# A streaming encoder step in split float32: hi and lo part of an operand as one 512-column moving operand in the first half of the tokens

## Chip, cores, metric

The kernel runs on one core of one Trainium2 chip. The metric is device time in microseconds. The kernel before took 2561.59 us, the median of 3 runs (2561.55 to 2563.88).

## What is computed

One inference step of an encoder with model width 1024 for 512 prompt tokens and 32 sample tokens, all float32. There are two layers, and each is a SwiGLU feed-forward network (FFN), a token mixer, and a second FFN, with RMSNorm and modulation around each:

```python
x = x + HALF * mod[:, 2, None] * rms_norm(swiglu(h, w_ffn_in[l, 0], w_ffn_out[l, 0]), g_norm[l, 1])
...   # the mixer: retention in layer 0, differential attention in layer 1
x = x + HALF * mod[:, 8, None] * rms_norm(swiglu(h, w_ffn_in[l, 1], w_ffn_out[l, 1]), g_norm[l, 5])
...   # after layer 0: one shared K/V projection of x

def swiglu(h, w_in, w_out):
    a, b = jnp.split(h @ w_in, 2, axis=-1)
    return (jax.nn.silu(a) * b) @ w_out
```

`w_ffn_in` is 1024 x 5632, `w_ffn_out` 2816 x 1024. Retention has a 1024 x 6144 input and a 2048 x 1024 output projection, K/V 1024 x 2048, the attention's query and output 1024 x 1024 each. The modulation vectors `mod` come from matrix-vector products with 1024 x 9216 weights for each layer.

## The kernel before

**Layout.** Activations lie transposed, features on the 128 partitions and tokens along the free dimension. The 544 tokens are cut into two halves, H = 0 with 256 columns and H = 1 with 288 (`COLS`, L28). Both halves go through all stages.

**Split float32.** A product of float32 values is made of three fp32r matmuls: a weight is split into w_hi (a cast, L578) and w_lo (the rest, L581), an operand into x_hi and x_lo (for instance L929 and L930), and w_hi x_hi + w_hi x_lo + w_lo x_hi is accumulated in one PSUM bank.

**Units.** A unit is one block of 128 output features with 6 or 8 k-tiles of 128 input features. There are 368 units in program order: 272 in the four FFNs, 64 in retention, 16 in shared K/V, 8 for queries, 8 for the attention's output. `run_unit` (L587) runs one unit for one half: per k-tile it waits for the operand (L593) and issues three matmuls at L599. Then the unit's `post` process takes the result from the bank and gives the bank back (`put_bank`). A half's run of an 8-tile unit is 24 matmuls. The `post` processes are: in an FFN `post_a` (Silu at L953 for layer 0, Tanh and a multiply at L949 and L950 for layer 1) and `post_b` (L965 or L962, then `split_ops`, L929 and L930); in `out_stage` a ScalarE copy (L916) for the first third of the inner dimension and a VectorE add (L918) for the others; rotary products (`rot`, L1021 and L1025); copies of values (L1074, L1375); gates (L1095). An FFN runs in three parts: 8, 8 and 6 pairs of `post_a` and `post_b` units, each followed by 8 output units that need the operands of that part.

**Memory.** Operand parts lie in `SLOT` (L346): 34 tiles for each half, of 256 or 288 columns, and an operand takes two of them (L686). Everything else of changing life is cut from an arena `FA` of 20600 columns. Banks: 5 of 8 for units (`MAINB`), 3 for the rest. Four weight buffers (`NW`), three for raw weights (`NRAW`).

**Order.** `Sched` simulates the engines with assumed costs (`c_r`, `c_act`, `c_dvp` and others, L243) and so fixes, before the launch, the order in which each engine's instructions are issued. Where several are ready, the lowest priority number goes first: post processes have 20 or 15, normalisation 1 to 2 (`x_norm`, `pre_ops`), a unit's matmuls 1000 plus their place in the order, the modulation matmuls (L504) `ADA_HI` = 900 once their due unit is reached, weight casts and subtractions `CONV_P` and `FIN_P` = 0.

`plan` (L636) merges the two halves' units into one order of 736 places along a path. A pair (a, b) of the path says how many units the first and the second half have done. The path is set by hand: `BND` (L62) at the joins between sub-layers up to layer 1's first FFN, `ATT` (L64) from there on, both in offsets from a stage's first unit. Mostly the halves alternate, the first one unit ahead; near joins it is some units ahead, and in layer 1 up to some 60. `plan` also decides on weight loads: where the halves of a unit are close together, one load and one split serve both (`Load(u, 2)`), elsewhere each half loads its own. `launch` (L621) goes through the order, waits for the unit's split weights, and takes a bank.

**Joins.** After the last output unit of a sub-layer, `sub_end` (L845) makes squares (L824), their sum (L828), a mean over partitions by TensorE (L711), a power on GpSimd (L717), a broadcast by TensorE (L722), the scaled sum into X (L877, L880), and `x_norm` and `pre_ops` make the next operands (L749, L758, L764). Meanwhile TensorE has the other half's units.

All loads and stores are DMAs issued by SyncE (`nc.sync`, L394). The rotary tables are loaded when unit `ROPE_LEAD` = 30 before the stage is launched.

Of the kernel before, what the change touches and what calls it, by code (L numbers as in the profile page):

```python
# [49 lines left out]
def _path():  # L50
# [3 lines left out]
    for e in ((0, 1), (0, 2), "kv", (1, 0)):  # L54
# [216 lines left out]
class Operand:  # L271
# [51 lines left out]
def yoco_step(ctx: ExitStack, tc: tile.TileContext, I, O):  # L323
# [19 lines left out]
    NHALF = sb("NHALF", [P, 4])  # L343
    LAM = sb("LAM", [P, 12])
    GSUB = sb("GSUB", [P, 1])
    SLOT = [[sb(f"r{H}_{i}", [P, COLS[H].stop - COLS[H].start], F32R) for i in range(NSLOT[H])] for H in range(2)]  # L346
    WT = [sb(f"w{i}", [P, 2, 8, P], F32R) for i in range(NW)]
    AN = ARENA_N
    FA = sb("FA", [P, AN])
# [237 lines left out]
    def run_unit(u, H, b):  # L587
        c = COLS[H]
        n = c.stop - c.start
        d = u.load[H]  # L590
        for k in range(u.nk):
            op = u.ops[k]
            yield op.ev[H]  # L593

            def mm(k=k, op=op):
                hi, lo = op.hi(H), op.lo(H)
                w = WT[d.w]
                for j, (a, x) in enumerate(((0, hi), (0, lo), (1, hi))):
                    te.matmul(PS[b][:, :n], lhsT=w[:, a, k, :], rhs=x,  # L599
                                     start=(k == 0 and j == 0), stop=(k == u.nk - 1 and j == 2))  # L600
            yield pe(3 * c_r(n), mm)
        d.users -= 1
        if d.users == 0:
            S.put(wpool, d.w)
        u.stage.left[H] -= 1
        if u.stage.left[H] == 0:
            for op in u.stage.ops:
                for t in op.part[H]:
                    S.put(slots[H], t)
        go(u.post(H, b), 20)  # L610
# [71 lines left out]
    def ensure(op, H):  # L682
        if op.part[H] is None:
            if op.asked[H] is None:
                op.asked[H] = Ev()
                op.part[H] = yield ("get", slots[H], 2)  # L686
                S.set(op.asked[H])
            else:
                yield op.asked[H]
# [243 lines left out]
    def ffn(l, j, hops, yevs):  # L933
        w_in, w_out = I["w_ffn_in"][l][j], I["w_ffn_out"][l][j]
        parts = ((0, 8), (8, 16), (16, 22))
        for pi, (f0, f1) in enumerate(parts):
            st = Stage(hops if pi == 2 else [])
            gops = [Operand() for _ in range(f1 - f0)]
            for f in range(f0, f1):
                sil = {}  # L940
                sev = (Ev(), Ev())

                def post_a(H, b, sil=sil, sev=sev):
                    n = COLS[H].stop - COLS[H].start
                    t = yield from get(n)
                    sil[H] = t
                    if l in TANH:

                        yield act(n, lambda: nc.scalar.activation(fa(t), PS[b][:, :n], AF.Tanh, scale=0.5))  # L949
                        yield dvp(n, lambda: nc.vector.scalar_tensor_tensor(fa(t), fa(t), 1.0, PS[b][:, :n], ALU.add,  # L950
                                                                            ALU.mult))
                    else:
                        yield act(n, lambda: nc.scalar.activation(fa(t), PS[b][:, :n], AF.Silu))  # L953
                    put_bank(b)
                    S.set(sev[H])

                def post_b(H, b, sil=sil, sev=sev, op=gops[f - f0]):
                    n = COLS[H].stop - COLS[H].start
                    yield sev[H]
                    t = sil[H]  # L960
                    if l in TANH:
                        yield dvp(n, lambda: nc.vector.scalar_tensor_tensor(fa(t), PS[b][:, :n], 0.5, fa(t), ALU.mult,  # L962
                                                                            ALU.mult))
                    else:
                        yield dvp(n, lambda: nc.vector.tensor_tensor(fa(t), PS[b][:, :n], fa(t), ALU.mult))  # L965
                    put_bank(b)
# [47 lines left out]
    def rot(H, b, rr, dst, pr=20, m=0):  # L1014
# [6 lines left out]
        yield dvp(n, lambda: nc.vector.tensor_tensor(a1, PS[b][:, :n], fa(rr, n, c.start), ALU.mult), pr)  # L1021

        def sw():
            for x, y in ((0, 64), (64, 0)):
                nc.vector.tensor_tensor(fa(t1, n, n, x, x + 64), PS[b][y:y + 64, :n],  # L1025
                                        fa(rr, n, NTOK + c.start, y, y + 64), ALU.mult)
        yield ("DVE", 2 * c_dvp(n), sw, pr)
        put_bank(b)
# [11 lines left out]
    def retention(hops, yevs):  # L1040
# [8 lines left out]
        for h in range(8):  # L1049
# [40 lines left out]
            def post_g(H, b, hd=hd, h=h, j=0):  # L1090
# [262 lines left out]
    def shared_kv(hops):  # L1353
# [3 lines left out]
        for h in range(8):  # L1357
# [604 lines left out]
```

## Time and profile before

| | |
|---|---|
| median of 3 runs | 2561.59 us (2561.55 to 2563.88) |
| the profiled execution | 2562.68 us |
| its span, first to last instruction | 2560.9 us |
| mean granted TensorE clock | 0.993 |
| instructions | 48166 |
| matmul instructions, of them at L599 | 19848, 17280 |
| DMA | 404.61 MB, mean 158 GB/s |

The profile is of one execution, taken by the hardware. PE is TensorE's matmuls, PEld its weight loads (they overlap PE), DVE is VectorE, ACT ScalarE, POOL GpSimd, SP SyncE. Matmuls are pipelined, so one's duration overlaps the next one's. In tiles' names `ps` is a PSUM bank, `w` a split weight buffer, `r` an operand part, `FA` the arena. A clock of 1.00 is the full 2.4 GHz, 0.5 is 1.2 GHz.

### The profile page before, as it was taken

How to read it: one execution, taken by the hardware profiler on the slowest of the kernel's cores; microseconds unless marked ns; L12 is line 12 of the kernel's file. 1: busy time of each engine (PE TensorE's matmuls, PEld its weight loads, DVE VectorE, ACT ScalarE, POOL GpSimd, SP SyncE). 2: the span in 40 equal slices, each digit the busy share in tenths (PEclk: the TensorE clock that was granted, in tenths of full speed). 3: DMA queues.
4: the chain of work that ended last, by engine and by line, in shares of the span. 5: the costliest groups of instructions: out<-in, count | busy, mean ns of one | idle time of the engine just before them, and what ended most of it. 6: DMA issues, size and time to landing. Idle time of an engine off the chain costs nothing.

```text
span 2560.9 us, 48166 instructions
## 1 busy us (share of the span) xinstructions
PE 2496.2 (97%) x19848; PEld 2379.2 (93%) x19848; DVE 1400.1 (55%) x2604; ACT 1091.3 (43%) x2159; POOL 58.5 (2%) x88
## 2 busy tenths in 40 slices
PE   7999999999999999999999999999899999999998
PEld 5889999899999997999998899999699988898998
DVE  5223334955424457323338944555786987768555
ACT  4222224643333355322126533444565655465434
POOL 0000000000000000000000000000000000000000
PEclk9999999999999999999999999999899999999999
DMA  8662323642222237522226853555655445545553
GB/s 321 263 239 84 98 90 107 227 152 95 80 80 91 76 109 279 189 88 95 91 76 221 271 173 127 167 180 190 241 194 175 159 160 185 178 161 169 165 165 109
DMA packets 122235, 404.61 MB, mean 158 GB/s; under 512 B 15008, under 2 KB 33568, under 8 KB 111776
## 3 DMA queue, kind: packets, MB, share of 16 engines
q1 hardware_dynamic: 122016, 401.54, 45.9%
q8 instruction: 155, 2.54, 0.4%
q14 instruction: 64, 0.52, 0.1%
HBM read 388.25 MB, written 13.24 MB: 157 GB/s over the span
## 4 chain that ended last, share of the span: by engine, by line
PE 86%; DVE 8%; ACT 3%; issue 2%; DMA 1%; POOL 0%; SPq 0%; POOLq 0%; DVEq 0%; ACTq 0%
PE ps L599 77%; DVE w L581 2%; PE ps L504 2%; ACT w L578 1%; DVE FA L1025 1%; DVE FA L749 1%; DVE r L764 1%; PE ps L1601 1%; PE ps L1231 1%; PE ps L1219 1%; ACT FA L858 0%; PE ps L1540 0%; DMA X<-in_xb 0%; PE ps L1594 0%; DVE FA L828 0%
## 5 line engine op out<-in xcount | busy, mean ns | idle before, releaser
L599 PE MATMUL ps<-r,w 128*128 128x256 f32 (+1 forms) x17280 | 2269.4, 291 | 15.8 <-ACT r L758 11.5
L599 PEld LDWEIGHTS ps<-r,w 128*128 128x128 f32 x17280 | 2205.5, 191 | 55.7 <-issue 25.9
L581 DVE TENSOR_TENSOR w<-FA,w 128x1024 fp32r<-128x1024 f32 (+1 forms) x552 | 658.9, 1194 | 572.4 <-ACT w L578 567.5
L578 ACT CAST w<-FA 128x1024 fp32r<-128x1024 f32 (+1 forms) x552 | 564.6, 1023 | 883.5 <-PE ps L599 799.8
L965 DVE TENSOR_TENSOR FA<-ps,FA 128x256 f32<-128x256 f32 (+1 forms) x88 | 38.8, 441 | 192.5 <-PE ps L599 191.9
L929 ACT CAST r<-FA 128x288 fp32r<-128x288 f32 (+1 forms) x176 | 73.1, 416 | 107.3 <-DVE FA L965 88.3
L918 DVE TENSOR_TENSOR FA<-ps,FA 128x288 f32<-128x288 f32 (+1 forms) x144 | 62.3, 438 | 97.7 <-PE ps L599 96.2
L930 DVE TENSOR_TENSOR r<-FA,r 128x288 fp32r<-128x288 f32 (+1 forms) x176 | 76.6, 437 | 21.9 <-ACT r L929 21.5
L758 ACT ACTIVATE r<-FA,MOD 128x256 fp32r<-128x256 f32 (+1 forms) x168 | 63.1, 437 | 51.7 <-DVE FA L749 51.3
L828 DVE TENSOR_TENSOR FA<-FA 128x256 f32<-128x256 f32 (+1 forms) x168 | 73.1, 436 | 12.7 <-ACT FA L824 11.1
L504 PE MATMUL ps<-FA,SC 128*32 128x512 f32 x576 | 70.7, 605 | 5.6 <-DMA FA<-in_ada 5.6
L962 DVE SCALAR_TENSOR_TENSOR FA<-ps,FA 128x288 f32<-128x288 f32 (+1 forms) x88 | 38.4, 439 | 49.9 <-PE ps L599 49.8
L953 ACT ACTIVATE FA<-ps 128x256 f32<-128x256 f32 (+1 forms) x88 | 34.5, 393 | 69.7 <-PE ps L599 69.6
L749 DVE SCALAR_TENSOR_TENSOR FA<-X,DRV,ps 128x256 f32<-128x256 f32 (+1 forms) x168 | 57.3, 396 | 9.5 <-PE ps L722 9.3
L717 POOL TENSOR_TENSOR FA<-FA,NHALF 128x2 f32<-128x2 f32 (+1 forms) x24 | 21.7, 906 | 1774.8 <-DVE FA L715 1687.0
L858 ACT ACTIVATE FA<-FA,DRV 128x256 f32<-128x256 f32 (+1 forms) x144 | 59.1, 442 | 2.9
L764 DVE SCALAR_TENSOR_TENSOR r<-FA,MOD,r 128x256 fp32r<-128x256 f32 (+1 forms) x168 | 58.5, 400 | 0.4 <-ACT r L758 0.2
L1025 DVE TENSOR_TENSOR FA<-ps,FA 64x288 f32<-64x288 f32 (+1 forms) x128 | 56.1, 438 | 2.0
L916 ACT COPY FA<-ps 128x288 f32<-128x288 f32 (+1 forms) x96 | 36.3, 380 | 44.6 <-PE ps L599 44.6
L1021 DVE TENSOR_TENSOR FA<-ps,FA 128x256 f32<-128x256 f32 (+1 forms) x64 | 27.8, 437 | 48.9 <-PE ps L599 48.8
L504 PEld LDWEIGHTS ps<-FA,SC 128*32 128x32 f32 x576 | 14.8, 109 | 33.6 <-issue 22.4
L824 ACT ACTIVATE FA<-FA 128x256 f32<-128x256 f32 (+1 forms) x84 | 35.7, 425 | 15.5 <-DVE FA L918 14.9
(149 smaller groups left out, 1120.6 us busy)
## 6 DMA issues: line engine op xcount, KB each, us to landing
FA<-in_w_ffn_in SPq DMA_DIRECT2D x261, 512.0 KB, 3.3
FA<-in_ada SPq DMA_DIRECT2D x80, 1024.0 KB, 7.1
FA<-in_w_ffn_out SPq DMA_DIRECT2D x95, 512.0 KB, 3.5
FA<-in_w_in_a SPq DMA_DIRECT2D x58, 512.0 KB, 3.2
FA<-in_w_ffn_out SPq DMA_DIRECT2D x62, 384.0 KB, 3.1
FA<-in_w_kv SPq DMA_DIRECT2D x24, 512.0 KB, 4.4
FA<-in_w_out_a SPq DMA_DIRECT2D x20, 512.0 KB, 3.6
FA<-in_w_q_b SPq DMA_DIRECT2D x16, 512.0 KB, 3.4
```

The source lines that it names most:

```text
L504: te.matmul(PS[b][32 * g:32 * g + 32, :], lhsT=SC[:, k, :], rhs=fa(ada_buf[u, k], 512, g * 512), start=(k == 0), stop=(k == 7))
L578: yield act(n, lambda: nc.scalar.copy(hi, src))
L581: yield dve(n, lambda: nc.vector.tensor_tensor(lo, src, hi.bitcast(F32), ALU.subtract))
L599: te.matmul(PS[b][:, :n], lhsT=w[:, a, k, :], rhs=x, start=(k == 0 and j == 0), stop=(k == u.nk - 1 and j == 2))
L749: nc.vector.scalar_tensor_tensor(fa(z, c1 - c0, o), X[:, f, c0:c1], DRV[:, gi, f, s:s + 1], PS[Rb][:, o:o + c1 - c0], ALU.mult, ALU.mult)
L758: nc.scalar.activation(op.hi(H, c0, c1), fa(z, c1 - c0, o), AF.Identity, bias=MOD[:, mi, f, s:s + 1])
L764: nc.vector.scalar_tensor_tensor(op.lo(H, c0, c1), fa(z, c1 - c0, o), MOD[:, mi, f, s:s + 1], op.hi(H, c0, c1).bitcast(F32), ALU.add, ALU. ...
L828: yield dve(n, lambda: nc.vector.tensor_tensor(acc, acc, fa(t), ALU.add))
L918: yield dvp(n, lambda: nc.vector.tensor_tensor(Y[:, f, c], PS[b][:, :n], Y[:, f, c], ALU.add), 15)
L929: yield act(n, lambda: nc.scalar.copy(op.hi(H), src), pr)
L930: yield dve(n, lambda: nc.vector.tensor_tensor(op.lo(H), src, op.hi(H).bitcast(F32), ALU.subtract), pr)
L1025: nc.vector.tensor_tensor(fa(t1, n, n, x, x + 64), PS[b][y:y + 64, :n], fa(rr, n, NTOK + c.start, y, y + 64), ALU.mult)
```

## The change

In the first half (H = 0) the two parts of an operand lie side by side in one tile of 2 x 256 columns. Per k-tile, one matmul of w_hi takes both as a moving operand of 512 columns, and one matmul of w_lo takes x_hi with 256 columns. A bank then holds two partial results. `result` adds them: a ScalarE copy of the right half, then a VectorE add of the left half. `out_stage` past the first third adds both halves to its target with two VectorE adds. The post processes of H = 0 work on the sum in the arena. H = 1 is as before. The offsets of the order, the number of slots (17 double ones in place of 34), and some priorities and leads are set anew.

```diff
-BND = {(0, 1): (7, 7, 6, 10), (0, 2): (7, 7, 6, 5), 'kv': (8, 8, 6, 8), (1, 0): (0, 1, 4, 6)}
+BND = {(0, 1): (7, 7, 7, 12), (0, 2): (8, 9, 10, 7), 'kv': (8, 9, 10, 8), (1, 0): (7, 0, 4, 0)}
-ATT = [(Q, -67, Q, -75), (Q, 4, Q, -34), (Q, 8, Q, -23), (OB, 0, Q, -31), (OB, -8, Q, -13), (F2, 1, Q, -16),
-       (F2, -6, Q, 0), (F2, 6, Q, -2), (F2, 37, OB, -1), (F2, 55, OB, 1), (F2, 55, F2, 0), (F2, 70, F2, -4)]
-NSLOT = (34, 34)
+ATT = [(Q, -64, Q, -67), (Q, 0, Q, -40), (Q, 8, Q, -24), (OB, -16, Q, -32), (OB, -8, Q, -18), (F2, 1, Q, -26),
+       (F2, -12, Q, 0), (F2, 7, Q, 0), (F2, 26, OB, -2), (F2, 59, OB, 3), (F2, 47, F2, 1), (F2, 73, F2, -5)]
+NSLOT = (17, 17)
...
             def mm(k=k, op=op):
-                hi, lo = op.hi(H), op.lo(H)
                 w = WT[d.w]
-                for j, (a, x) in enumerate(((0, hi), (0, lo), (1, hi))):
-                    te.matmul(PS[b][:, :n], lhsT=w[:, a, k, :], rhs=x,
-                                     start=(k == 0 and j == 0), stop=(k == u.nk - 1 and j == 2))
-            yield pe(3 * c_r(n), mm)
+                first, last = k == 0, k == u.nk - 1
+                if H:
+                    for j, (a, x) in enumerate(((0, op.hi(H)), (0, op.lo(H)), (1, op.hi(H)))):
+                        te.matmul(PS[b][:, :n], lhsT=w[:, a, k, :], rhs=x, start=first and j == 0,
+                                  stop=last and j == 2)
+                else:
+                    te.matmul(PS[b][:], lhsT=w[:, 0, k, :], rhs=op.part[H][:].rearrange("p s n -> p (s n)"),
+                              start=first, stop=False)
+                    te.matmul(PS[b][:, :n], lhsT=w[:, 1, k, :], rhs=op.hi(H), start=False, stop=last)
+            yield pe(3 * c_r(n) if H else c_r(n) + c_r(2 * n), mm)
...
+    def result(b, dst, pr=None):
+
+        yield act(256, lambda: nc.scalar.copy(dst, PS[b][:, 256:]), pr)
+        yield dvp(256, lambda: nc.vector.tensor_tensor(dst, PS[b][:, :256], dst, ALU.add), pr)
+        put_bank(b)
...
-                if first:
-                    yield act(n, lambda: nc.scalar.copy(Y[:, f, c], PS[b][:, :n]), 15)
+                if H == 0 and first:
+                    yield from result(b, Y[:, f, c], 15)
                 else:
-                    yield dvp(n, lambda: nc.vector.tensor_tensor(Y[:, f, c], PS[b][:, :n], Y[:, f, c], ALU.add), 15)
-                put_bank(b)
+                    if first:
+                        yield act(n, lambda: nc.scalar.copy(Y[:, f, c], PS[b][:, :n]), 15)
+                    else:
+                        def add():
+                            for o in range(0, 512 - 256 * H, 256):
+                                nc.vector.tensor_tensor(Y[:, f, c], PS[b][:, o:o + n], Y[:, f, c], ALU.add)
+                        yield ("DVE", (2 - H) * c_dvp(n), add, 15)
+                    put_bank(b)
...
                 def post_a(H, b, sil=sil, sev=sev):
                     n = COLS[H].stop - COLS[H].start
                     t = yield from get(n)
                     sil[H] = t
+                    src = PS[b][:, :n]
+                    if H == 0:
+                        s = yield from get(n)
+                        src = fa(s)
+                        yield from result(b, src)
...
-ROPE_LEAD = 30
+ROPE_LEAD = 38
...
-FIN_P = 0
-CONV_P = 0
+FIN_P = 1.05
+CONV_P = 1.05
...
-ADA_HI = 900
+ADA_HI = 1100
...
-ADA_LEAD = -52
+ADA_LEAD = -66
```

`post_b`, `rot`, `post_v`, `post_g` and `post_k` begin in the same way as `post_a` for H = 0: `result` into a piece of the arena, then what they did before, on that piece in place of the bank. In `post_v` of retention and of the shared K/V, `result` stands in place of the ScalarE copy.

## Rows read from the trace of the kernel before

**Rows 1.** Part 1 of the page: busy time, share of the span and instructions of each engine.
```profile
PE 2496.2 (97%) x19848; PEld 2379.2 (93%) x19848; DVE 1400.1 (55%) x2604; ACT 1091.3 (43%) x2159; POOL 58.5 (2%) x88
```
**Rows 2.** Part 4 of the page: the chain that ended last, share of the span by engine and by line.
```profile
PE 86%; DVE 8%; ACT 3%; issue 2%; DMA 1%; POOL 0%; SPq 0%; POOLq 0%; DVEq 0%; ACTq 0%
PE ps L599 77%; DVE w L581 2%; PE ps L504 2%; ACT w L578 1%; DVE FA L1025 1%; DVE FA L749 1%; DVE r L764 1%; PE ps L1601 1%; PE ps L1231 1%; PE ps L1219 1%; ACT FA L858 0%; PE ps L1540 0%; DMA X<-in_xb 0%; PE ps L1594 0%; DVE FA L828 0%
```
**Rows 3.** Who waited for whom, whole span: us in total, times, longest us. First ScalarE's longest wait, then TensorE's six longest.
```profile
ACT w L578 <- PE ps L599: 799.8, 410, 5.8
...
PE ps L711 <- DVE FA L828: 15.0, 6, 11.2
PE ps L599 <- ACT r L758: 11.5, 5, 5.3
PE ps L504 <- DMA FA<-in_ada: 5.6, 3, 2.7
PE ps L1119 <- DVE FA L1030: 5.5, 13, 1.0
PE ps L722 <- POOL FA L717: 4.8, 7, 1.3
PE ps L599 <- DVE r L764: 4.0, 8, 0.7
```
**Rows 4.** The matmuls of L599 in two stretches in which only one shape runs, 1950.6 to 1973 us and 2345 to 2547 us: count, duration in ns (least, median, greatest), starts of the first and the last in us, shape and most frequent form.
```profile
L599 PE MATMUL ps<-r,w x190: 280/283/284, 1950.3 to 1973.0; 128*128 128x256 f32 x190
...
L599 PE MATMUL ps<-r,w x1530: 288/294/301, 2344.8 to 2546.9; 128*128 128x288 f32 x192
```
**Rows 5.** Groups of instructions with shapes kept apart, whole span: busy us and mean ns of one, then idle time before them and who ended it.
```profile
L599 PE MATMUL ps<-r,w 128*128 128x288 f32 x8640 | 1226.2, 297 | 3.3 <-ACT r L758 1.7 <-DVE r L764 1.4
L599 PE MATMUL ps<-r,w 128*128 128x256 f32 x8640 | 1116.4, 286 | 12.5 <-ACT r L758 9.8 <-DVE r L764 2.6
L504 PE MATMUL ps<-FA,SC 128*32 128x512 f32 x576 | 70.7, 605 | 5.6 <-DMA FA<-in_ada 5.6
```
**Rows 6.** Timeline of TensorE in a retention head: start us, busy us, line, shape, count.
```profile
523.86 0.59 PE L1219 MATMUL ps<-FA 128*128 128x256 f32 x2
524.29 0.59 PE L1218 MATMUL ps<-FA 128*128 128x256 f32 x2
524.72 0.59 PE L1219 MATMUL ps<-FA 128*128 128x256 f32 x2
525.15 0.60 PE L1221 MATMUL ps<-FA 128*128 128x256 f32 x2
525.59 0.59 PE L1279 MATMUL ps<-FA 128*128 128x256 f32 x2
526.02 0.59 PE L1280 MATMUL ps<-FA 128*128 128x256 f32 x2
```
**Rows 7.** Groups with shapes kept apart, as in rows 5: operations on 256 columns that take results from a bank, and the split of an operand.
```profile
L918 DVE TENSOR_TENSOR FA<-ps,FA 128x256 f32<-128x256 f32 x72 | 30.3, 423 | 32.8 <-PE ps L599 31.5
L916 ACT COPY FA<-ps 128x256 f32<-128x256 f32 x48 | 17.5, 369 | 44.6 <-PE ps L599 44.6
L965 DVE TENSOR_TENSOR FA<-ps,FA 128x256 f32<-128x256 f32 x44 | 18.7, 424 | 27.3 <-PE ps L599 26.8 <-ACT FA L953 0.6
L930 DVE TENSOR_TENSOR r<-FA,r 128x256 fp32r<-128x256 f32 x88 | 37.0, 422 | 21.3 <-ACT r L929 21.0
L929 ACT CAST r<-FA 128x256 fp32r<-128x256 f32 x88 | 35.5, 404 | 102.5 <-DVE FA L965 85.4 <-DVE FA L962 17.1
```
**Rows 8.** Timeline of VectorE: three adds of L918 in a row at 2331.64 us (start us, busy us, line, shape, count).
```profile
2331.64 1.07 DVE L918 TENSOR_TENSOR FA<-ps,FA 128x256 f32<-128x256 f32 x3
```
**Rows 9.** Weight preparation, groups as in rows 5, and from the DMA view the loads of the modulation weights (count, KB each, median us from issue to landing).
```profile
L581 DVE TENSOR_TENSOR w<-FA,w 128x1024 fp32r<-128x1024 f32 x490 | 599.8, 1224 | 552.6 <-ACT w L578 547.7 <-DMA FA<-in_w_ffn_in 2.3 <-DMA FA<-ksc 0.5
L578 ACT CAST w<-FA 128x1024 fp32r<-128x1024 f32 x490 | 513.2, 1047 | 841.3 <-PE ps L599 757.8 <-issue 59.6 <-DMA FA<-in_w_ffn_in 11.5
L581 DVE TENSOR_TENSOR w<-FA,w 128x768 fp32r<-128x768 f32 x62 | 59.2, 955 | 19.8 <-ACT w L578 19.8
L578 ACT CAST w<-FA 128x768 fp32r<-128x768 f32 x62 | 51.5, 830 | 42.2 <-PE ps L599 42.0
...
FA<-in_ada SPq DMA_DIRECT2D x80, 1024.0 KB, 7.1
```
**Rows 10.** Two stretches around joins in layer 1: length in us, busy us and count for PE, PEld, DVE, ACT, POOL, then granted clock, DMA share and GB/s.
```profile
1800.00:1825.00 25.00, 17.30 (x131) 11.90 (x130) 18.42 (x40) 9.55 (x21) 1.38 (x2) 0.73 0.63 241
2315.00:2340.00 25.00, 19.65 (x141) 19.33 (x141) 21.83 (x55) 17.20 (x38) 0.85 (x1) 0.86 0.44 144
```
**Rows 11.** The stretch 2000 to 2100 us: columns as in rows 10, then its group of 256-column matmuls (as in rows 5).
```profile
2000.00:2100.00 100.00, 98.44 (x804) 91.25 (x803) 89.70 (x192) 63.95 (x141) 4.16 (x6) 1.00 0.50 165
...
L599 PE MATMUL ps<-r,w 128*128 128x256 f32 x482 | 62.6, 285 | 0.0
```

More of the change, by code (lines that the diff above doesn't have):

```diff
@@ L285, in _at @@
     def _at(self, i, H, c0, c1):
-        t = self.part[H][i]
+        t = self.part[H]
         if c0 is None:
-            return t[:]
+            return t[:, i]
         o = COLS[H].start
-        return t[:, c0 - o:c1 - o]
+        return t[:, i, c0 - o:c1 - o]
 class Unit:
@@ L345, in yoco_step @@
     GSUB = sb("GSUB", [P, 1])
-    SLOT = [[sb(f"r{H}_{i}", [P, COLS[H].stop - COLS[H].start], F32R) for i in range(NSLOT[H])] for H in range(2)]
+    SLOT = [[sb(f"r{H}_{i}", [P, 2, COLS[H].stop - COLS[H].start], F32R) for i in range(NSLOT[H])] for H in range(2)]
     WT = [sb(f"w{i}", [P, 2, 8, P], F32R) for i in range(NW)]
@@ L607, in run_unit @@
             for op in u.stage.ops:
-                for t in op.part[H]:
-                    S.put(slots[H], t)
+                S.put(slots[H], op.part[H])
         go(u.post(H, b), 20)
+    def result(b, dst, pr=None):
+        yield act(256, lambda: nc.scalar.copy(dst, PS[b][:, 256:]), pr)
+        yield dvp(256, lambda: nc.vector.tensor_tensor(dst, PS[b][:, :256], dst, ALU.add), pr)
+        put_bank(b)
     order = []
@@ L685, in ensure @@
                 op.asked[H] = Ev()
-                op.part[H] = yield ("get", slots[H], 2)
+                op.part[H] = (yield ("get", slots[H], 1))[0]
                 S.set(op.asked[H])
@@ L946, in post_a @@
                     sil[H] = t
+                    src = PS[b][:, :n]
[3 more added lines that the diff above has]
+                        yield from result(b, src)
                     if l in TANH:
-                        yield act(n, lambda: nc.scalar.activation(fa(t), PS[b][:, :n], AF.Tanh, scale=0.5))
-                        yield dvp(n, lambda: nc.vector.scalar_tensor_tensor(fa(t), fa(t), 1.0, PS[b][:, :n], ALU.add,
-                                                                            ALU.mult))
-                    else:
-                        yield act(n, lambda: nc.scalar.activation(fa(t), PS[b][:, :n], AF.Silu))
-                    put_bank(b)
+                        yield act(n, lambda: nc.scalar.activation(fa(t), src, AF.Tanh, scale=0.5))
+                        yield dvp(n, lambda: nc.vector.scalar_tensor_tensor(fa(t), fa(t), 1.0, src, ALU.add, ALU.mult))
+                    else:
+                        yield act(n, lambda: nc.scalar.activation(fa(t), src, AF.Silu))
+                    if H:
+                        put_bank(b)
+                    else:
+                        free(s)
                     S.set(sev[H])
@@ L958, in post_b @@
                     n = COLS[H].stop - COLS[H].start
+                    src = PS[b][:, :n]
+                    if H == 0:
+                        s = yield from get(n)
+                        src = fa(s)
+                        yield from result(b, src)
                     yield sev[H]
@@ L1020, in rot @@
         a1, a2 = fa(t1, n), fa(t1, n, n)
-        yield dvp(n, lambda: nc.vector.tensor_tensor(a1, PS[b][:, :n], fa(rr, n, c.start), ALU.mult), pr)
+        src = PS[b][:, :n]
+        if H == 0:
+            s = yield from get(n)
+            src = fa(s)
+            yield from result(b, src, pr)
+        yield dvp(n, lambda: nc.vector.tensor_tensor(a1, src, fa(rr, n, c.start), ALU.mult), pr)
         def sw():
             for x, y in ((0, 64), (64, 0)):
-                nc.vector.tensor_tensor(fa(t1, n, n, x, x + 64), PS[b][y:y + 64, :n],
+                nc.vector.tensor_tensor(fa(t1, n, n, x, x + 64), src[y:y + 64],
                                         fa(rr, n, NTOK + c.start, y, y + 64), ALU.mult)
         yield ("DVE", 2 * c_dvp(n), sw, pr)
-        put_bank(b)
+        if H:
+            put_bank(b)
+        else:
+            free(s)
         if m < n:
@@ L1073, in post_v @@
                 t = yield from get(n)
-                yield act(n, lambda: nc.scalar.copy(fa(t), PS[b][:, :n]))
-                put_bank(b)
+                if H:
+                    yield act(n, lambda: nc.scalar.copy(fa(t), PS[b][:, :n]))
+                    put_bank(b)
+                else:
+                    yield from result(b, fa(t))
                 b2 = yield from bank(miscb)
@@ L1094, in post_g @@
                 dst = fa(hd.v["g"], NTOK, j * NTOK)[:, c]
-                yield act(n, lambda: nc.scalar.activation(dst, PS[b][:, :n], AF.Silu))
-                put_bank(b)
+                if H:
+                    yield act(n, lambda: nc.scalar.activation(dst, PS[b][:, :n], AF.Silu))
+                    put_bank(b)
+                else:
+                    yield from result(b, dst)
+                    yield act(n, lambda: nc.scalar.activation(dst, dst, AF.Silu))
                 S.set(hd.g[H])
@@ L1374, in post_v @@
                 t = yield from get(n)
-                yield act(n, lambda: nc.scalar.copy(fa(t), PS[b][:, :n]))
-                put_bank(b)
+                if H:
+                    yield act(n, lambda: nc.scalar.copy(fa(t), PS[b][:, :n]))
+                    put_bank(b)
+                else:
+                    yield from result(b, fa(t))
                 yield from to_tok(H, fa(t), h)
```

10 lines of the change are left out of this document (6 added, 4 removed).

## Prediction, made before the changed kernel ran

> **What bounds the kernel now.** I read the page's busy shares first: TensorE is busy 97% of the span, VectorE 55%, ScalarE 43% [rows 1]. A busy TensorE alone proves little, so next the chain of waits: 86% of it is TensorE, 77% the matmuls of L599, and weight preparation (L581, L578) is 3% [rows 2]. Then who releases whom. TensorE's longest waits are all at joins between sub-layers (L711, L722, L758) and none is for a weight; ScalarE's cast L578 on the other hand waits 799.8 us in all for TensorE to hand back a weight buffer [rows 3]. So weights are ready ahead of need, and what counts is how fast L599 goes, plus some idle time at joins.
>
> The pace comes from stretches of one kind. 190 matmuls of 256 columns start between 1950.3 and 1973.0 us: 22.7/189 = **120.1 ns** each. 1530 of 288 columns start between 2344.8 and 2546.9 us: 202.1/1529 = **132.2 ns** [rows 4]. The mean durations, 286 and 297 ns, are not the pace, since neighbours overlap. There are 8640 of each [rows 5]; at these paces they take 1037.7 + 1142.2 = 2179.9 us of 2560.9.
>
> **Matmuls.** The first half's 8640 are 2880 k-tiles of three. Now one k-tile is w_hi, w_hi, w_lo, three matmuls of 256: 360.3 ns. After, it is one of 512 and one of 256. The 256 stays at 120.1. No row has a 512-column matmul of this type, so I bound it. Lower end: a straight line through the two rows, 12.1 ns for 32 columns, gives 120.1 + 256 x 0.378 = 216.9 ns. The f32 matmuls of L1218 and L1219 back this end: five pairs from 523.86 to 526.02, 216 ns an instruction [rows 6]. But they are of another type. Upper end: cost goes by columns alone, 2 x 120.1 = 240.2. Between: at the granted clock of 1.00, that is 2.4 GHz, 256 columns at one per clock are 106.7 ns and 288 are 120.0, so 13.4 and 12.2 ns are there per matmul; 512 columns with 12.2 are 213.3 + 12.2 = **225.5 ns**. I take this one: it rests on the same line and type, where the excess hardly moves between 256 and 288. A k-tile is then 345.6 ns, 14.7 less, and 2880 x 14.7 = **42.3 us** go. The ends give 2880 x 23.3 = 67.1 us and 0. Below nothing I see no reason: it would take a 512 slower than its two halves. The 2880 weight loads that go had no time of their own: they overlap matmuls, so they are inside the pace.
>
> TensorE: Matmul & The Clock Gate of the Trainium skill, Back-to-back issue gap, puts the distance of matmuls at N/2.4 plus about 2.5 ns. By that a k-tile would go from 327.5 to 325.0 ns, an estimate that saves 7 us in all. The trace does not agree at 256 columns, 120.1 ns against 109.2 [rows 4].
>
> **Evacuation.** Each of the 368 first-half units gets one more VectorE add of 256 columns, priced by L918's 423 ns: 155.7 us. 224 of them (88 post_a, 88 post_b, 32 rotary, 16 gates) also get a ScalarE copy, by L916's 369 ns: 82.7 us [rows 7]. The others had a copy already or add twice. VectorE goes from 1400 to 1556 us, ScalarE from 1091 to 1174. On the path they cost nothing where L599 of the other half runs: a second-half unit is 24 x 132.2 = 3.17 us. The tight spot is an FFN part's end, where post_b's chain becomes about 0.37 + 0.42 + 0.42 + 0.40 + 0.42 = 2.03 us and hand-overs [rows 7]. Its cover is that 3.17 us unit, and the operand is wanted only at the last k-tile of the next first-half unit, 7 x 0.346 = 2.4 us later. Were the cover gone, each of 12 part ends would show up to 2 us. Banks are held about 0.8 us longer; five banks at 2.8 us a unit bear it.
>
> At a join the last output unit gets a second add. Back to back they come every 0.33 us (three in 1.07 [rows 8]), alone 0.42. Five joins and some hand-overs: I take **+3 us**, bounds 0 and 20.
>
> **Order and loads.** Walking the plan with the old offsets gives 552 weight loads (490 and 62, as in [rows 9]); with the new ones 569, that is 508 of 1024 and 61 of 768 columns. The 18 more and one fewer cost VectorE 18 x 1.224 - 0.955 = 21.1 us, ScalarE 18.0 us, and 9 MB of SP-queue transfers. They come two to four a stage from the first FFN to layer 1's first FFN. I cost them at nothing: buffers are the wait, not weights [rows 3]. Without that cover each would cost at most its 2.3 us of cast and subtract, 39 us for 17.
>
> Conversions drop in priority from 0 to 1.05, so they go behind the first normalised operand at a join; the same slack covers them. If it is gone, the launch behind them waits, and TensorE with it. The modulation matmuls (L504, 70.7 us [rows 5]) stay as many, but go behind the first 100 unit runs of the order, and later due dates move 14 units ahead. 100 runs of about 24 x 126 ns end near 40 + 303 = 343 us. The join at about 440 us needs two of their units, 16 loads of 1 MB at 7.1 us to landing [rows 9], two buffers deep: about 57 us at best, 114 one by one. So they should be in time; were they not, that join would wait up to 20 us, which is inside the bounds of the leads below. TensorE waits for these loads 5.6 us now [rows 3]. The rotary tables load 8 units earlier on the same queue; two transfers, nothing. The new leads at joins can take back idle time or add some. Idle time and half clock around 1800 to 1825 and 2315 to 2340 show what is at stake: TensorE idle 7.7 and 5.4 us with granted clocks 0.73 and 0.86 [rows 10]. I take 0, bounds -15 and +20.
>
> **Sum.** The profiled execution took 2562.7 us (span 2560.9 and 1.8 around it). 2562.7 - 42.3 + 3 = 2523.4. It is 1.1 above the median of 2561.59, so the forecast on that scale is **2522 us**.
>
> **Rivals.** (a) The 512-column matmul goes at the line's 216.9 ns: 67.1 us less, 2562.7 - 67.1 + 3 - 1.1 = 2497.5. For it: the excess falls from 13.4 to 12.2, and the f32 pace [rows 4, 6]. Against: 32 columns are a short lever. Chance 0.22.
> (b) Cost per matmul is only 2.7 ns (216 less the 213.3 of an f32 instruction [rows 6]) and the rest goes with columns: 2880 x 2.7 = 7.8 us, 2556.8, no measurable change. This is the case in which the merge does not do what it says, and the skill's estimate above comes out near it. Against: by it 288 columns would take 2.7 + 288 x 117.4/256 = 134.8, not 132.2. Chance 0.05.
> (c) Slower: the joins lose more than matmuls gain. The new leads and the later first-half results leave TensorE without work at each of the five joins as it now is at 1800 to 1825, and the clock falls. That place costs 7.7 us of idle time and 25 x (1 - 0.73) = 6.8 us by its clock [rows 10], some 14.5. A mean loss of 8.5 us more per join eats the gain; at 14.5 on top the time is 2562.7 - 42.3 + 72.5 - 1.1 = 2591.8. For it: VectorE is already at 89.7 of 100 us from 2000 to 2100, where 482 matmuls, 20 first-half units, would add 8.5 us [rows 11]. Against: in that very stretch TensorE is idle 1.6 us. Chance 0.08.
> (d) The same at a third of the price: 24 us lost in place of 3, 2543. Chance 0.09.
>
> **How the numbers follow.** My forecast has 0.56. A measurement of this kernel tells 0.2%, 5.1 us, from no change. Forecast, (a) and (d) are faster: 0.87. (b) gives 0.05 for the same. (c) gives 0.08. The range runs from 2490, (a) with 8 us of join time taken back, to 2550, (d) with its spread; it leaves out (b), (c) and the far tails of the rest.
>
> **What would show it.** In the profile after, 2880 matmuls of 512 and 2880 of 256 columns from the first half, in one stretch 345.6 ns a pair. 337 means (a), 357 means (b). VectorE near 1577 us, ScalarE near 1192, with 569 casts. TensorE's waits at L711, L722 and L758 about as now; if they exceed 40 us more, or the half clock shows at most joins, (c). What would prove me wrong: pairs at 346 ns and yet no gain, or TensorE waiting for w or for L581.

## The result, and the profile after

The changed kernel takes 2532.91 us in the median of 4 runs (2531.81 to 2534.82), against 2561.57 of the kernel before beside it: 0.9888 of its time, interval 0.9871 to 0.9905, or 28.7 us less. The forecast was 2522, 11 us too low; the range of 2490 to 2550 holds the time. The profiled execution took 2533.88 us, with a span of 2531.9 and a mean granted clock of 0.992.

First the busy times, answering to [rows 1]:

```profile
PE 2466.4 (97%) x16968; PEld 2213.0 (87%) x16968; DVE 1556.6 (61%) x2989; ACT 1184.1 (47%) x2400; POOL 62.1 (2%) x88
```

There are 2880 matmuls and weight loads fewer. TensorE is still 97% busy, so it lost as large a share as before although its work shrank. VectorE was forecast near 1577 and ScalarE near 1192; VectorE has some 20 us less than that. The chain that ended last, answering to [rows 2], keeps its 86% of TensorE; L599 has become L600 (second half), L603 (the 512-column matmul) and L605:

```profile
PE 86%; DVE 9%; ACT 2%; issue 2%; DMA 1%; POOL 0%; SPq 0%; DVEq 0%; POOLq 0%; ACTq 0%
PE ps L600 42%; PE ps L603 23%; PE ps L605 11%; DVE w L581 3%; PE ps L504 2%; DVE FA L759 1%; ACT w L578 1%; DVE r L774 1%; DVE FA L838 1%; DVE FA L1060 1%; PE ps L1649 1%; PE ps L1276 1%; PE ps L1264 1%; PE ps L1588 0%; PE ps L1642 0%
```

Groups with shapes kept apart, answering to [rows 5, 7, 9]: busy us, mean ns of one, then the idle time before them and who ended it. L618 and L619 are the copy and the add of `result`.

```profile
L600 PE MATMUL ps<-r,w 128*128 128x288 f32 x8640 | 1222.6, 297 | 4.7 <-DVE w L581 1.7 <-DVE FA L971 1.2 <-ACT r L768 1.1
L603 PE MATMUL ps<-r,w 128*128 128x512 f32 x2880 | 1045.2, 403 | 17.3 <-DVE r L774 7.1 <-DVE r L946 6.4 <-DVE FA L619 3.3
L605 PE MATMUL ps<-r,w 128*128 128x256 f32 x2880 | 805.2, 280 | 2.2 <-DVE w L581 1.7 <-DVE FA L1666 0.6
L581 DVE TENSOR_TENSOR w<-FA,w 128x1024 fp32r<-128x1024 f32 x508 | 621.8, 1224 | 445.5 <-ACT w L578 442.2
L619 DVE TENSOR_TENSOR FA<-ps,FA 128x256 f32<-128x256 f32 x296 | 123.1, 420 | 113.1 <-ACT FA L618 112.5
L618 ACT COPY FA<-ps 128x256 f32<-128x256 f32 x296 | 108.8, 368 | 219.5 <-PE ps L605 204.7 <-DVE FA L1068 12.8 <-issue 1.6
...
L933 DVE TENSOR_TENSOR FA<-ps,FA 128x256 f32<-128x256 f32 x144 | 60.7, 423 | 30.8 <-PE ps L605 28.2
L581 DVE TENSOR_TENSOR w<-FA,w 128x768 fp32r<-128x768 f32 x61 | 58.0, 953 | 14.2 <-ACT w L578 14.1
```

There are 508 and 61 weight casts, as counted from the plan. VectorE has 368 more adds, 296 at L619 and 72 at L933; the latter come in pairs.

**The pace.** First and last start of the 512-column matmuls in two stretches where each alternates with one of 256:

```profile
L603 PE MATMUL ps<-r,w x64: 392/394/395, 1898.0 to 1919.9; 128*128 128x512 f32 x64
...
L603 PE MATMUL ps<-r,w x56: 393/398/403, 916.6 to 936.0; 128*128 128x512 f32 x56
```

21.9/63 = 347.6 ns a pair in the one, 19.4/55 = 352.7 in the other. Of some 250 first-half units that ran without a break, about 190 are within 1 ns of 347 and some 40 at 352 to 354. The forecast was 345.6.

**The waits.** TensorE's, whole span, answering to [rows 3]: us in total, times, longest us.

```profile
PE ps L721 <- DVE FA L838: 14.5, 5, 11.4
PE ps L603 <- DVE r L774: 7.1, 5, 4.4
PE ps L603 <- DVE r L946: 6.4, 1, 6.4
PE ps L732 <- POOL FA L727: 4.2, 7, 1.3
PE ps L603 <- DVE FA L619: 3.3, 3, 2.3
...
PE ps L504 <- DMA FA<-in_ada: 0.2, 1, 0.2
```

L721 and L732 (L711 and L722 before) wait about as long as they did, and the wait for modulation weights is down to 0.2 us. One wait of 6.4 us for a split (L946) is new. The windows, answering to [rows 10], the first a long one for later, the others around this wait, show its second price, the clock:

```profile
2030.00:2330.00 300.00, 286.97 (x1880) 236.11 (x1879) 238.58 (x512) 173.43 (x390) 16.70 (x23) 0.98 0.51 164
2270.00:2278.00 8.00, 8.00 (x67) 6.87 (x66) 5.03 (x9) 4.38 (x10) 1.45 (x1) 1.00 0.50 146
2278.00:2286.00 8.00, 1.56 (x7) 1.09 (x7) 7.46 (x16) 3.29 (x9) 0.00 (x0) 0.75 0.01 4
2286.00:2296.00 10.00, 7.76 (x42) 5.84 (x41) 7.05 (x19) 5.85 (x13) 2.71 (x1) 0.52 0.25 79
```

TensorE's timeline there (start us, busy us): before the wait a 512-column matmul is busy 0.40 us, after it 0.80.

```profile
2278.29 0.40 PE L603 MATMUL ps<-r,w 128*128 128x512 f32 x1
2278.53 0.28 PE L605 MATMUL ps<-r,w 128*128 128x256 f32 x1
2285.25 0.80 PE L603 MATMUL ps<-r,w 128*128 128x512 f32 x1 [6.44 <-DVE r L946]
2285.85 0.41 PE L605 MATMUL ps<-r,w 128*128 128x256 f32 x1
```

**Work and lost time.** One account holds all kernels side by side. From the profiled execution of each: idle is its span less TensorE's busy time; clock is span x (1 - mean granted clock); lost is their sum; work is the span less lost. The clock has three digits, so lost is good to about 1.3 us by rounding alone. Idle time at the lower clock counts in both terms, which makes lost too large and work too small by 5 to 11 us in every kernel. Each line is also one execution: the granted clock of one kernel differs between its runs by up to 0.004 (e5_no_add has 0.993 to 0.996), some 10 us of the clock column, while the times of a kernel differ by up to 7. The profiled run of e1_split, 2557.11 us, lies 4.6 above the median; the others lie within 3.1 of theirs. Kernels with the same matmuls differ in work by up to 6. So a few us of lost time tell nothing by themselves. The ratios are to the kernel before as it ran beside each, at 2561.57 to 2562.94 us.

| kernel | median us | ratio to before (95%) | idle | clock | lost | work |
|---|---|---|---|---|---|---|
| before | 2561.57 | | 64.7 | 17.9 | 82.6 | 2478.3 |
| after | 2532.91 | 0.9888 (0.9871 to 0.9905) | 65.5 | 20.3 | 85.8 | 2446.1 |
| e1_split | 2552.53 | 0.9964 (0.9951 to 0.9978) | 60.1 | 17.9 | 78.0 | 2477.2 |
| e2_all512 | 2812.12, one run | | 50.9 | 14.1 | 65.0 | 2745.1 |
| e3_old_leads | 2559.09 | 0.9984 (0.9975 to 0.9994) | 81.6 | 25.6 | 107.2 | 2451.0 |
| e4_new_leads | 2548.27 | 0.9942 (0.9927 to 0.9957) | 55.6 | 10.2 | 65.8 | 2479.0 |
| e5_no_add | 2520.14 | 0.9833 (0.9820 to 0.9847) | 58.0 | 10.1 | 68.1 | 2449.1 |
| e6_f60 | 2531.95 | 0.9878 (0.9865 to 0.9892) | 63.8 | 15.2 | 79.0 | 2452.1 |
| e7_split_first | 2555.43 | 0.9970 (0.9958 to 0.9982) | 75.5 | 30.7 | 106.2 | 2450.6 |
| e8_old_order | 2566.75 | 1.0012 (1.0003 to 1.0021) | 87.5 | 28.2 | 115.7 | 2446.0 |
| e9_first276 | 2525.45 | 0.9858 (0.9844 to 0.9873) | 55.1 | 10.1 | 65.2 | 2459.7 |
| e10_last92 | 2555.96 | 0.9978 (0.9968 to 0.9987) | 66.0 | 10.2 | 76.2 | 2476.1 |

### The profile page after: what moved, and what is told of

Same layout as the page of the kernel before. It is cut to its first block, busy times and chain, and to the rows that moved or that the text cites. A ratio compares the mean times of both kernels' runs of the same rounds, so it can differ in the third digit from the quotient of the medians.

```text
span 2531.9 us, 43008 instructions
## 1 busy us (share of the span) xinstructions
PE 2466.4 (97%) x16968; PEld 2213.0 (87%) x16968; DVE 1556.6 (61%) x2989; ACT 1184.1 (47%) x2400; POOL 62.1 (2%) x88
## 4 chain that ended last, share of the span: by engine, by line
PE 86%; DVE 9%; ACT 2%; issue 2%; DMA 1%; POOL 0%; SPq 0%; DVEq 0%; POOLq 0%; ACTq 0%
PE ps L600 42%; PE ps L603 23%; PE ps L605 11%; DVE w L581 3%; PE ps L504 2%; DVE FA L759 1%; ACT w L578 1%; DVE r L774 1%; DVE FA L838 1%; DVE FA L1060 1%; PE ps L1649 1%; PE ps L1276 1%; PE ps L1264 1%; PE ps L1588 0%; PE ps L1642 0%
## 5 line engine op out<-in xcount | busy, mean ns | idle before, releaser
L600 PE MATMUL ps<-r,w 128*128 128x288 f32 x8640 | 1222.6, 297 | 4.7 <-DVE w L581 1.7
L600 PEld LDWEIGHTS ps<-r,w 128*128 128x128 f32 x8640 | 1161.3, 189 | 35.0 <-issue 14.4
L603 PE MATMUL ps<-r,w 128*128 128x512 f32 x2880 | 1045.2, 403 | 17.3 <-DVE r L774 7.1
L581 DVE TENSOR_TENSOR w<-FA,w 128x1024 fp32r<-128x1024 f32 (+1 forms) x569 | 679.7, 1195 | 459.7 <-ACT w L578 456.3
L578 ACT CAST w<-FA 128x1024 fp32r<-128x1024 f32 (+1 forms) x569 | 582.5, 1024 | 711.3 <-PE ps L600 510.8
L605 PE MATMUL ps<-r,w 128*128 128x256 f32 x2880 | 805.2, 280 | 2.2 <-DVE w L581 1.7
L603 PEld LDWEIGHTS ps<-r,w 128*128 128x128 f32 x2880 | 543.8, 189 | 149.1 <-issue 13.4
L605 PEld LDWEIGHTS ps<-r,w 128*128 128x128 f32 x2880 | 545.6, 189 | 3.7 <-DVE w L581 2.5
L618 ACT COPY FA<-ps 128x256 f32<-128x256 f32 x296 | 108.8, 368 | 219.5 <-PE ps L605 204.7
L619 DVE TENSOR_TENSOR FA<-ps,FA 128x256 f32<-128x256 f32 x296 | 123.1, 420 | 113.1 <-ACT FA L618 112.5
L933 DVE TENSOR_TENSOR FA<-ps,FA 128x256 f32<-128x256 f32 (+1 forms) x216 | 93.0, 434 | 86.0 <-PE ps L600 55.1
L945 ACT CAST r<-FA 128x256 fp32r<-128x256 f32 (+1 forms) x176 | 73.3, 417 | 72.7 <-DVE FA L992 40.9
L946 DVE TENSOR_TENSOR r<-FA,r 128x256 fp32r<-128x256 f32 (+1 forms) x176 | 76.7, 436 | 24.1 <-ACT r L945 23.4
L838 DVE TENSOR_TENSOR FA<-FA 128x288 f32<-128x288 f32 (+1 forms) x168 | 72.9, 435 | 12.0 <-ACT FA L834 10.6
L504 PE MATMUL ps<-FA,SC 128*32 128x512 f32 x576 | 69.5, 598 | 0.2 <-DMA FA<-in_ada 0.2
```

The costliest lines, as they stand in the source:

```text
L504: te.matmul(PS[b][32 * g:32 * g + 32, :], lhsT=SC[:, k, :], rhs=fa(ada_buf[u, k], 512, g * 512), start=(k == 0), stop=(k == 7))
L578: yield act(n, lambda: nc.scalar.copy(hi, src))
L581: yield dve(n, lambda: nc.vector.tensor_tensor(lo, src, hi.bitcast(F32), ALU.subtract))
L600: te.matmul(PS[b][:, :n], lhsT=w[:, a, k, :], rhs=x, start=first and j == 0, stop=last and j == 2)
L603: te.matmul(PS[b][:], lhsT=w[:, 0, k, :], rhs=op.part[H][:].rearrange("p s n -> p (s n)"), start=first, stop=False)
L605: te.matmul(PS[b][:, :n], lhsT=w[:, 1, k, :], rhs=op.hi(H), start=False, stop=last)
```

## The experiments

**e1_split**: the changed kernel, but from a unit's second k-tile on (2512 of 2880) the 512-column matmul is two of 256 into the two halves of the bank. Order, evacuation and leads stay.

```diff
-te.matmul(PS[b][:], lhsT=w[:, 0, k, :], rhs=<both parts>, start=first, stop=False)
+if first:
+    te.matmul(PS[b][:], lhsT=w[:, 0, k, :], rhs=<both parts>, start=True, stop=False)
+else:
+    te.matmul(PS[b][:, :n], lhsT=w[:, 0, k, :], rhs=op.hi(H), start=False, stop=False)
+    te.matmul(PS[b][:, n:], lhsT=w[:, 0, k, :], rhs=op.lo(H), start=False, stop=False)
```

> Undoes the merge alone: from the second k-tile of a unit on (2512 of 2880) the 512-column matmul is again two of 256, into the two halves of the bank; evacuation, order and leads are those of the changed kernel, and the engines' order is the same. Theory M (the gain is the merged matmul's): a split k-tile goes back from 347.1 to 3 x 120.1 = 360.3 ns, 2512 x 13.2 = 33 us, so 2566 us. Rival L (the gain is the new order's and leads'): stays within 8 us of 2533.

Measured 2552.53 us (2550.04 to 2557.37), 19.6 above the changed kernel: between the two expectations, so neither came true. In the account work rises by 31.1 us, as the slower matmuls should make it, and lost time falls by 7.8. So the merge does save matmul time, and part of it comes back as waiting. That a slower TensorE hides more of what the other engines do would fit this; no run tests it apart.

**e2_all512**: the w_lo matmul takes both parts too, so the first half has matmuls of 512 columns alone. It computes w_lo x_lo in addition.

```diff
-te.matmul(PS[b][:], lhsT=w[:, 0, k, :], rhs=<both parts>, start=first, stop=False)
-te.matmul(PS[b][:, :n], lhsT=w[:, 1, k, :], rhs=op.hi(H), start=False, stop=last)
+for a in range(2):
+    te.matmul(PS[b][:], lhsT=w[:, a, k, :], rhs=<both parts>, start=first and a == 0, stop=last and a == 1)
```

> Measures a 512-column matmul by itself: the w_lo matmul takes both operand parts too (it adds the product of w_lo and x_lo), so the first half has only 512-column matmuls, two a k-tile. A fixed 13.4 ns a matmul over 213.3: a pair takes 453.4 ns, some 306 us more than the changed kernel, 2839 us. The straight line through 256 and 288 columns: 433.8 ns, 2783 us. The 231.5 ns that separate a 512 from the next 256 in the changed kernel, taken as its own cost: 463 ns, 2867 us.

Its matmuls of L604 in a stretch where no others run, columns as in [rows 4]:

```profile
L604 PE MATMUL ps<-r,w x127: 389/389/393, 2118.6 to 2147.2; 128*128 128x512 f32 x127
```

28.6/126 = **227.0 ns** for one 512-column matmul, two of them 454: the pace of the fixed cost. The total, 2812 us, is 27 under what that theory gave for it: lost time is 65.0 us in place of 85.8, which fits the same reason. It is one run.

**e3_old_leads**: the changed kernel with all settings of before (`BND`, `ATT`, `ROPE_LEAD` 30, `FIN_P` and `CONV_P` 0, `ADA_HI` 900, `ADA_LEAD` -52), so merge and evacuation alone. **e4_new_leads**: the kernel before with all of those set as after, so the settings alone.

> The changed matmuls and evacuation with all offsets, priorities and leads of before (552 loads). Theory M: the new settings are worth little, 2525 to 2541 us. Rival L (the later first-half results need the new leads, or the gain is theirs): joins lose as much as the merge gains, 2555 us or more.

> The kernel before with the new offsets, priorities and leads and nothing else (569 loads). Theory M: within 10 us of before, 2552 to 2572 us. Rival L: it gains most of the 29 us, 2535 to 2545 us.

e3 takes 2559.09 us against 2562.81 beside it: merge and evacuation alone gain 3.7 us (interval of the ratio 0.9975 to 0.9994), as rival L had it. Its work is 27.3 us less than before, and its lost time 24.6 more. e4 takes 2548.27, between its two expectations: the settings alone gain 14.5 us, in lost time (82.6 to 65.8), with the old matmuls. On the new ones the same settings give 2559.1 - 2532.9 = 26.2. I had put them at nothing.

**e5_no_add**: the VectorE adds of the two partial results are left out, and the ScalarE copy takes the left half; the term w_hi x_lo is thus missing from the first half. Matmuls, copies, order and settings stay.

```diff
-yield act(256, lambda: nc.scalar.copy(dst, PS[b][:, 256:]), pr)
-yield dvp(256, lambda: nc.vector.tensor_tensor(dst, PS[b][:, :256], dst, ALU.add), pr)
+yield act(256, lambda: nc.scalar.copy(dst, PS[b][:, :256]), pr)
+yield dvp(256, lambda: None, pr)
...
-for o in range(0, 512 - 256 * H, 256):
+for o in range(0, 256, 256):
```

> The changed kernel without the 368 VectorE adds that join the two halves of a bank: the result takes the left half alone, so w_hi x_lo is left out of the first half's sums. The ScalarE copy stays, the order of all other instructions too. Theory E (the adds cost time on the path, because operands and banks come later): some 15 us less, 2515 to 2522 us. Rival S (the adds are covered, and the time given back comes from TensorE running faster against the same joins): within 5 us of the changed kernel, 2528 to 2538 us.

Measured 2520.14 us (2518.38 to 2523.14), 12.8 under the changed kernel. VectorE is 138.9 us less busy (1556.6 to 1417.7), 377 ns an add. TensorE's work is the same within 3 us; lost time falls by 17.7, of which 10.2 is clock in the profiled runs (over four runs of each the clock is 0.992 to 0.994 with the adds, 0.993 to 0.996 without). The large named waits stay (for L946 still 6.4, L721 still 14.5); what goes is spread over the joins. So the adds cost about 13 us, where I had 3 for all of the evacuation, although VectorE is idle 39% of the span with them. Each engine's order is kept, so what the merge changes in the order, and what the copies cost, is not in these 13.

**e6_f60**: one point of the path moved by one unit, aimed at the 6.4 us wait alone.

```diff
-(F2, 59, OB, 3)
+(F2, 60, OB, 3)
```

> The changed kernel with one offset of the order moved, (F2, 59, OB, 3) to (F2, 60, OB, 3): the last post_b unit of the first half runs before the second half's six units of the join instead of after them, so its split is not queued behind the second half's normalisation. Theory Q (the 6.4 us wait at 2278 us and the half clock behind it are that queue): 6.4 us and about 6.8 us of clock go, less some 2 us of cover, 2520 to 2527 us. Rival C (the join lacks cover anyway): 2530 to 2538 us.

2531.95 us (ratio 0.9878, interval 0.9865 to 0.9892): no gain that can be told, as rival C had it. The wait is gone, and others stand in its place; TensorE's waits from 2200 to 2330 us:

```profile
PE ps L603 <- DVE FA L933: 4.7, 1, 4.7
PE ps L600 <- DVE FA L971: 3.8, 1, 3.8
PE ps L600 <- ACT r L768: 2.2, 1, 2.2
```

**e7_split_first**: the first half's splits get a priority ahead of the normalisation (0.95 in place of 20), since VectorE works through the second half's sums while TensorE waits for L946. VectorE's timeline in the changed kernel (start us, busy us) shows that queue:

```profile
2282.48 0.75 DVE L890 TENSOR_TENSOR X<-X,FA 128x576 f32<-128x576 f32 x1
2283.15 0.45 DVE L838 TENSOR_TENSOR FA<-FA 128x288 f32<-128x288 f32 x1
2283.52 0.41 DVE L990 SCALAR_TENSOR_TENSOR FA<-FA 128x256 f32<-128x256 f32 x1
2283.85 1.01 DVE L838 TENSOR_TENSOR FA<-FA 128x288 f32<-128x288 f32 x2
2284.78 0.42 DVE L946 TENSOR_TENSOR r<-FA,r 128x256 fp32r<-128x256 f32 x1
```

```diff
 def split_ops(H, src, op, pr=20):
+    pr = pr if H else 0.95
```

> The changed kernel with the first half's operand split in the FFNs (L945, L946) at priority 0.95, ahead of normalisation and weight preparation, in place of 20. Theory Q (first-half results queued behind normalisation at joins are what eats the gain): the 2278 us wait goes and some others shrink, 2518 to 2528 us. Rival C: normalisation and weights come later instead, 2532 us or more.

2555.43 us, 22.5 slower, and the wait stays (L946 is L947 here). TensorE also waits longer for weights, as rival C had it: 4.4 us for subtractions (L581; 1.7 in the changed kernel) and 3.9 for casts (L578):

```profile
PE ps L603 <- DVE r L947: 6.7, 2, 6.4
PE ps L605 <- DVE w L581: 4.4, 6, 0.9
...
PE ps L603 <- ACT w L578: 3.9, 4, 1.1
```

Lost time rises by 20.4 us, half of it clock. This does not settle theory Q, because the edit moved the wrong link. In the changed kernel it is the multiply ahead of the split (L990) that ran late, at 2283.52 us behind the sums; cast and subtraction followed it within 1.3 us. The edit leaves the multiply at priority 20, and here too (L991) it stands behind the same sums:

```profile
2306.54 0.45 DVE L838 TENSOR_TENSOR FA<-FA 128x288 f32<-128x288 f32 x1
2306.91 0.41 DVE L991 SCALAR_TENSOR_TENSOR FA<-FA 128x256 f32<-128x256 f32 x1
2307.24 1.01 DVE L838 TENSOR_TENSOR FA<-FA 128x288 f32<-128x288 f32 x2
2308.17 0.42 DVE L947 TENSOR_TENSOR r<-FA,r 128x256 fp32r<-128x256 f32 x1
```

No run gives the multiply another priority.

**e8_old_order**: the changed kernel with the old offsets (`BND`, `ATT`) alone; priorities and the other leads stay new.

> The changed kernel with the old offsets of the order and the new priorities and leads (552 loads). If the offsets are what the new settings bring: near the kernel with all old settings, 2552 to 2562 us. If it is the priorities and leads of modulation, conversion and rotary loads: near the changed kernel, 2530 to 2540 us.

2566.75 us: 34 slower than the changed kernel, and slower than the kernel before (1.0003 to 1.0021). Lost time is 115.7 us. That is above both expectations. The new priorities and leads bring nothing without the new offsets (e3, with none of the new settings, is 7.7 faster), and the offsets bring 34 us with them. The new offsets under the old priorities and leads were not run, so whether they count alone is not shown.

**e9_first276** and **e10_last92**: the changed kernel with the merge and its evacuation in the first 276 units of the program order alone, or in the last 92 alone (the attention's queries and output, the last FFN, and eight units ahead of them); the other units run as before, all with the new settings.

```diff
+both = H == 0 and u.idx < 276        # e10: u.idx >= 276
+merged[b] = both
...
-if H:
+if not both:
...
-if H == 0:
+if merged[b]:
```

> All new settings; the first half's 512-column matmuls and the sum behind them in units 0 to 275 alone. The last 92 units (the end of layer 1's first FFN, attention, last FFN: 704 of 2880 k-tiles, from about 1730 us) are as in the kernel before. Theory D (the gain is given back in this dense stretch): by the traces TensorE loses 56.6 us from 1700 us on in the changed kernel and 34.9 us in the kernel with new settings alone, while the 704 k-tiles gain 704 x 12.9 = 9.1 us; 12.6 us net go, 2520 us. Rival U (the loss is spread evenly, like the gain of 15.4 us): 704/2880 of it is missing, 2537 us.

> The other way round: new settings, 512-column matmuls in the last 92 units alone. Theory D: 12.6 us above the kernel with new settings alone, 2561 us. Rival U: 3.8 us below it, 2544 us.

e9 takes **2525.45 us** (2524.17 to 2526.69): it beats both kernels, the changed one by 7.5. e10 takes 2555.96, 7.7 above e4, which merges nothing. So in the last 92 units the merge costs about 7.5 us net whichever way it is asked. The effects add up: 2525.45 + 2555.96 - 2548.27 = 2533.1, and the changed kernel has 2532.9. The account shows it as lost time: e9 has 65.2, as e4 has 65.8, while e10 has 76.2. Its main place is the stretch from 2030 to 2330 us, here for e9, then e10, with TensorE's longest wait in it (columns as in [rows 10]; the spans differ, so the work in it is not quite the same):

```profile
2030.00:2330.00 300.00, 294.33 (x2339) 267.35 (x2338) 222.25 (x456) 164.67 (x359) 14.52 (x23) 0.99 0.54 168
...
PE ps L604 <- DVE FA L938: 3.9, 1, 3.9
```

```profile
2030.00:2330.00 300.00, 284.36 (x1822) 231.71 (x1823) 239.98 (x521) 173.85 (x394) 16.89 (x22) 0.98 0.51 161
...
PE ps L607 <- DVE r L951: 6.5, 1, 6.5
```

Idle time plus 300 x (1 - clock) is 5.7 + 3 us without the merge there, 15.6 + 6 with it, and VectorE goes from 222 to 240 us busy. With the merge the long wait for the split (L951 in e10) is there. In the changed kernel it is 13.0 + 6; in e8, with the old offsets, 21.4 + 15; in e5, without the adds, still 10.5 + 6. Here are e8, then e5:

```profile
2030.00:2330.00 300.00, 278.64 (x1753) 226.79 (x1754) 231.03 (x502) 164.27 (x377) 15.11 (x22) 0.95 0.49 152
...
2030.00:2330.00 300.00, 289.53 (x1934) 243.10 (x1933) 218.75 (x448) 171.02 (x381) 15.54 (x23) 0.98 0.52 166
```

So VectorE's load is not the whole cause in this stretch: e5 has no more of it than e9, 218.75 us against 222.25, and loses nearly twice as much, with the 6.4 us wait for the split still there. What makes up the rest, the copies, the longer chain or the order that the merge leads to, stays open.

## Why the prediction was right and wrong

**Right: what bounds, and the pace.** The kernel went as fast as its matmuls, and the 512-column matmul came out at the value I chose, with a fixed part per matmul: 227.0 ns measured, 225.5 forecast, between bounds of 216.9 and 240.2. Rivals (a) and (b) fall by that. 512 columns at one per clock are 213.3 ns, so 13.7 are there per matmul, as 13.4 at 256 and 12.2 at 288 [rows 4]. By TensorE: Matmul & The Clock Gate of the Trainium skill, Back-to-back issue gap, it would be 213.3 + 2.5 = 215.8, an estimate; the section gives this as the gap of an isolated matmul and says that in a stream of weight loads and matmuls both set the spacing. The stream here, at 227.0, is slower than that formula, as it was at 256 columns.

**Too large: 42.3 us for the merge.** At 347 ns a pair it is 2880 x (360.3 - 347) = 38.3, and the slower units at 353 take some 2 to 3 of it. In the account the six kernels with every k-tile merged in this way have 2446.0 to 2452.1 us of work, mean 2449, and the three with (nearly) none 2477.2 to 2479.0, mean 2478: 29 us. The paces thus promise some 36 and the account has 29, with its scatter of up to 6; what lies between stays open. This term is where the 11 us of the result come from: from before to after the account has 32.2 us less work and 3.2 us more lost time, and the forecast had 42.3 and 3.

**The first step that failed: "+3 us" for evacuation and joins.** Counts and single durations were right (368 adds, 420 to 423 ns each); in busy time an add weighs 377 ns, since neighbours overlap, so VectorE came to 1556.6 us and not 1577. Wrong was "on the path they cost nothing where L599 of the other half runs". Lost time rises with the merge by 24.6 us under the old settings (before to e3) and by 20.0 under the new (e4 to after); leaving out the adds alone takes 17.7 back. By the medians, with 29 us of work, the merge's loss is some 25 and 14, and the adds are 12.8 of the latter. I weighed one unit's chain against the 3.17 us that cover it. But e9 and e10 put much of the cost where VectorE is busy 80% of the time (238.58 of 300 us) and TensorE waits for it at several places, of which taking away one only brings out the next (e6). The adds are one part of that; in the same stretch e5 keeps most of the loss without them, and that part's cause is open. A long wait costs twice: after the 6.4 us the granted clock is 0.52 from 2286 to 2296 us, that is the lower level, 1.2 GHz. The bounds of 0 and 20 nearly held; the value did not.

**The second: "0" for the new leads.** They give 16.8 us of lost time on the old matmuls (before to e4) and 21.4 on the new (e3 to after), 14.5 and 26.2 in the medians. The bound was -15. Idle time and half clock at joins were there to be had [rows 10]; I read them as what could be lost as well, and took the middle. With the merge these two errors have opposite signs and about the same size: +24.6 - 21.4 by way of e3, +20.0 - 16.8 by way of e4, either way +3.2, where the forecast had +3 + 0. That they cancel was luck. Had the new settings really brought 0, the time would have been that of e3, 2559.09 us, outside the range.

**The rivals.** (c) had the mechanism right, joins where TensorE goes without work and a clock that falls, but at the wrong place and in part with the wrong culprit. It blamed the new leads beside the later results; the leads are what holds it down. Under the old offsets it shows in full: e8 loses 33.1 us more than before, under half of its 72.5, and it eats the whole gain of work, 32.3. (d), 24 us lost in place of 3, is nearly what e3 shows (24.6). (c) asked for VectorE's dense stretch from 2000 to 2100 us [rows 11]; the loss of the last 92 units is mostly in the same part of the program, from 2030 to 2330, though not by VectorE's load alone.

**The small ones.** Not all of TensorE's longest waits in [rows 3] are at joins, as the prediction read them: L504 waits 5.6 us for modulation weights, and L1119 5.5 us in the retention heads. The 17 extra weight loads cost nothing to be seen: e4 has them all and none of its TensorE's six longest waits is for L581; in the changed kernel these waits are 1.7 us at L600 and 1.7 at L605. The modulation weights came in time, 5.6 us of waiting became 0.2. L721 and L732 wait as L711 and L722 did.

## What to carry to other kernels

Cost a change that takes time from the bounding engine and gives work to others in two columns, the work that it removes and the time that the bounding engine will stand idle or at half clock; here, under the old order, the second took 24.6 of 27.3 us. It is found by the same merge under the old order and the same order without the merge. Where a hand-set order comes with a change, run it on the old code first: here the order alone gave 14.5 of the 28.7 us. And try the change in one part of the program at a time: leaving the merge out of the last 92 units was 7.5 us faster than making it everywhere. Before moving an instruction ahead in a queue, look in the timeline which one of its chain stands behind the others (e7).

## What the runs showed of the hardware that I had not expected

The same pair of matmuls, 512 and 256 columns with operands of the same kind, runs at 347 ns in most units and at 352 to 354 in some 40 of about 250; the cause stays open. An idle stretch of 6.4 us is followed by some ten us at the lower clock (granted 0.52 from 2286 to 2296 us), so a wait at a join costs more than itself: the 512-column matmul is busy 0.80 us right after it. And a slower TensorE lost less: with 227 ns matmuls throughout the first half (e2, one run) lost time was 65.0 us, against 85.8.
